# The output projection of a gated decoder trunk: a plain tiled product, or a fifth stage of seven block products

## The chip, the core and the metric

The kernel runs on one NeuronCore of a Trainium2 chip. Its engines work side by side and are joined by semaphores: TensorE (PE, matrix products; PEld are its weight loads), VectorE (DVE), ScalarE (ACT), GpSimd (POOL) and SyncE (SP), which mostly issues transfers. The core has 16 DMA engines. The metric is the device time of one execution in microseconds (us): the median of the runs.

## The reference, cut to what matters

The sizes are T = 1024 tokens and D = 1024 channels, in fp32.

```python
mod = c_act @ ada_w[l] + ada_b[l]
shift, scale, gate = jnp.split(mod, 3, axis=-1)
h = rms_norm(x, norm_w[l]) * (1.0 + scale[:, None, :]) + shift[:, None, :]
proj = h @ w_in[l]
...
u_h = y_h @ w_branch[l, 0]
u_g = y_g @ w_branch[l, 1]
mg = jax.nn.sigmoid(mg.reshape(B, T, N_BRANCH, D_MODEL))
merged = mg[:, :, 0] * u_h + mg[:, :, 1] * u_g
x = x + gate[:, None, :] * (merged @ w_out[l])
...
return rms_norm(x, final_norm_w)
```

## The kernel before, in words

Every large product is made in three passes: each fp32 operand is split into a rounded part `hi` and a remainder `lo` (ACT casts, DVE subtracts; `split`, L195 and L196), and `hi*hi + hi*lo + lo*hi` is summed in PSUM.

The first 820 us or so compute the input projection and the two attention branches. Then come four **product stages**, numbered b = 0 to 3, of 1024 x 1024 x 1024 each: stages 0 and 1 compute the two merge gates `mg`, stages 2 and 3 the branch projections `u_g` and `u_h`. Each is written as a two-by-two block product with seven products of 512 x 512 x 512 instead of eight (Winograd's form of Strassen's method), in the order of `PRODUCTS` (1, 2, 5, 3, 6, 7, 4). A product has four row blocks i, each one PSUM bank of 128 x 512, with 4 x 3 = 12 matmuls in `Pair.run` (L1399). Sums and differences of the blocks are needed as operands: those of the activations are made by DVE from four **quarters** (`load_quad`, `combine`, `build`; `build` also splits, L1319 and L1320); those of the weights are made long before in a side job and kept in DRAM (`weight_sums`), read back by `load_duo` (L1330) and split by `prep_duo` (L1341, L1342), two row blocks ahead. Partial results stay in PSUM banks a, e and b, with copies in SBUF.

After a row block, `Pair.after` hands results to the stage's output function. Stage 3's is `put_m`, which multiplies by the gate (L1491) and adds the other branch (L1494): `merged` is done, channels on partitions.

The **output projection** is a plain product: `make_m` splits the merged halves into `m_hi` and `m_lo`, called after each row block of stage 3; `OutBlk` (two of them, one per 512 output columns) loads `w_out`, splits it in `prep`, and in `run` computes eight row blocks of 24 matmuls (L1169, L1170, L1171). After each row block DVE multiplies the bank by the output gate `gate_b` (L1174), adds it to the row of x (L1176), and ACT squares and sums it (L1178); in the second half the root mean square is completed (L1184 to L1186), both halves are scaled (L1187, L1189) and stored (L1188, L1190).

The order of the work is set by a list of hooks, `at`, filled by `after(b, p, i, f)`: f runs, in program order, after row block i of product p in stage b. PE's, ACT's and DVE's instructions are then ordered ahead of the run from this program by the framework; on the chip each engine takes them strictly in that order. SP and POOL issue transfers in order too. SBUF outside of constants is 46 buffers of 4 KB per partition (`Slots`), taken and returned first in, first out; a transfer into a returned buffer waits until its last reader is done.

Of the kernel before, what the change touches and what calls it, by code (L numbers as in the profile page):

```python
# [15 lines left out]
P = 128  # L16
D = 1024
# [13 lines left out]
SUMS = {5: 0, 6: 1, 3: 2, 7: 3}  # L31

# [50 lines left out]
def hybrid_trunk_kernel(  # L83
# [1055 lines left out]
    class OutBlk:  # L1139


        def __init__(self, half):
            self.half, self.sl = half, slice(half * 512, half * 512 + 512)

        def load(self):
            self.raw = []
            for kk in range(4):
                b = S.get([2, 512])
                nc.sync.dma_start(b, w_out[0, kk * 256:(kk + 1) * 256, self.sl].rearrange("(k p) f -> p k f", p=P))
                self.raw.append(b)  # L1150

        def prep(self):
            self.wt = []
            for b in self.raw:
                self.wt.append(split(b))
                S.free(b)

        def run(self, at):
            half, sl = self.half, self.sl
            for n, t in enumerate((4, 5, 6, 7, 0, 1, 2, 3)):  # L1160
                if half == 0:
                    xr[t] = load_x(t)
                if n in at:
                    at[n]()
                po = R.get()
                for k in range(KT):
                    hi, lo = self.wt[k // 2]
                    lh, ll = m_hi[k][:, t * P:(t + 1) * P], m_lo[k][:, t * P:(t + 1) * P]
                    nc.tensor.matmul(po, lh, hi[:, k % 2, :], start=(k == 0), stop=False)  # L1169
                    nc.tensor.matmul(po, lh, lo[:, k % 2, :], start=False, stop=False)  # L1170
                    nc.tensor.matmul(po, ll, hi[:, k % 2, :], start=False, stop=(k == KT - 1))  # L1171
                r = xr[t][:, sl]
                tmp = xb_f[:, (n % 2) * 512:(n % 2) * 512 + 512]
                nc.vector.tensor_mul(tmp, po, gate_b[0][:, sl])  # L1174
                R.free(po)
                nc.vector.tensor_add(r, r, tmp)  # L1176
                junk = xb_f[:, 1024 + (n % 2) * 512:1024 + (n % 2) * 512 + 512]
                nc.scalar.activation(junk, r, AF.Square, accum_out=sso[:, t, half:half + 1])  # L1178
                f = fnw[0]
                if half == 0:  # L1180
                    nc.vector.tensor_mul(r, r, f[:, sl])
                else:
                    rs = rso[:, t:t + 1]
                    nc.vector.tensor_add(rs, sso[:, t, 0:1], sso[:, t, 1:2])  # L1184
                    nc.scalar.activation(rs, rs, AF.Sqrt, bias=eps_t, scale=1.0 / D)
                    nc.vector.reciprocal(rs, rs)  # L1186
                    nc.scalar.activation(xr[t][:, 0:512], xr[t][:, 0:512], AF.Copy, scale=rs)  # L1187
                    nc.sync.dma_start(o2[t * P:(t + 1) * P, 0:512], xr[t][:, 0:512])  # L1188
                    nc.vector.scalar_tensor_tensor(r, r, rs, f[:, sl], ALU.mult, ALU.mult)  # L1189
                    nc.sync.dma_start(o2[t * P:(t + 1) * P, 512:1024], r)  # L1190
            for hi, lo in self.wt:
                S.free(hi, lo)

# [261 lines left out]
    def half_of(store, d, half):  # L1458
        if d not in store:
            store[d] = S.get([T])  # L1460
        return store[d][:, half * 512:half * 512 + 512]

    gate0, gate1 = {}, {}
    gate1_d = [dp.tile([P, T], F32, name=f"gate1_{d}") for d in range(8)]
    m_hi, m_lo = [None] * 8, [None] * 8
# [7 lines left out]
    def put_gate0(d, half, ap, summed):  # L1473
        nc.scalar.activation(half_of(gate0, d, half), ap, AF.Sigmoid)
        if summed:
            Q.free(ap)
# [5 lines left out]
    def put_t1(d, half, ap, summed):  # L1482
        g = half_of(gate1, d, half)
        nc.vector.tensor_mul(g, g, ap)
        if summed:
            Q.free(ap)

    def put_m(d, half, ap, summed):
        sl = slice(half * 512, half * 512 + 512)
        g = gate0[d][:, sl]  # L1490
        nc.vector.tensor_mul(g, g, ap)  # L1491
        if summed:
            Q.free(ap)
        nc.vector.tensor_add(g, g, gate1[d][:, sl])  # L1494
        if d % 2 or half:
            later.extend([(d, 0)] if d % 2 == 0 else [])
            later.append((d, half))

    later = deque()
    made = {}  # L1500

    def make_m(leave=0):
        while len(later) > leave:
            d, half = later.popleft()
            if m_hi[d] is None:
                m_hi[d], m_lo[d] = S.get([T], F32R), S.get([T], F32R)
            sl = slice(half * 512, half * 512 + 512)
            split(gate0[d][:, sl], m_hi[d][:, sl], m_lo[d][:, sl])
            made[d] = made.get(d, 0) + 1
            if made[d] == 2:  # L1510
                S.free(gate0.pop(d), gate1.pop(d))
# [16 lines left out]
    for p in PRODUCTS[1:]:  # L1528
        for i in range(4):
            after(3, p, i, lambda: make_m(1))  # L1530
# [96 lines left out]
```

## Time and profile before

| what | value |
| --- | --- |
| median of 3 runs | 1237.3 us (1235.79 to 1238.61) |
| the profiled execution, its own time | 1236.45 us |
| its span, first to last instruction | 1234.7 us |
| PE / DVE / ACT / POOL busy | 1199.6 / 759.7 / 533.0 / 116.4 us |
| product stage 1 (about 903 to 980 us) | DVE 34.0, ACT 37.5 us busy in 77 us |
| product stage 3 (about 1057 to 1138 us) | DVE 71.9, ACT 38.7 us busy in 81 us |
| output projection (from about 1138 us) | DVE 44.4, ACT 26.1 us busy in the 97 us to the end |
| HBM read, written | 125.53 MB, 41.94 MB |

The views quoted below: busy shares of the whole span; stretches of time with each engine's busy time and the number of its instructions (x); the timeline, with an instruction's start and length and, in brackets, the engine's idle time before it and what ended it; groups of instructions by line; and the chain of waits, followed back from the end. A matmul's length in the timeline overlaps its neighbours, so their distance is read from the chain.

### The profile page before, as it was taken

The numbers are of one execution on the slowest core, as the hardware profiler recorded it, in microseconds if no ns is written. First come the engines' busy times: TensorE is split into PE (matmuls) and PEld (weight loads), VectorE is DVE, ScalarE is ACT, GpSimd is POOL, SyncE is SP. The second block draws the span as 40 slices with busy tenths as digits, with TensorE's granted clock in tenths as the row PEclk, the third lists the DMA queues.
The fourth block names the chain that finished last, engine by engine and source line by source line (L and its number), as shares of the span: only waits on it lengthen the run. The fifth ranks groups of instructions, "written<-read, shape, count | busy, mean of one in ns | idle before, by whom it ended". The sixth has DMA issues, their size and how long they took to land.

```text
span 1234.7 us, 20836 instructions
## 1 busy us (share of the span) xinstructions
PE 1199.6 (97%) x8627; PEld 992.4 (80%) x8627; DVE 759.7 (62%) x1225; ACT 533.0 (43%) x785; POOL 116.4 (9%) x201
## 2 busy tenths in 40 slices
PE   5999999999999999999999999999999999998997
PEld 3777889899898888788878878877888887787786
DVE  4636344765938375787774276785432668979443
ACT  5547723344444333424523233457543534454222
POOL 4100000202111121021010101101100000000000
PEclk9999999999999999999999999999999999999999
DMA  9714001746452367255151111345547456235202
GB/s 324 263 68 137 18 18 37 283 126 212 137 166 101 108 224 239 64 195 174 46 188 50 52 52 52 103 138 201 166 163 240 152 185 189 75 97 186 104 35 102
DMA packets 126928, 168.82 MB, mean 137 GB/s; under 512 B 7019, under 2 KB 97185, under 8 KB 126834
## 3 DMA queue, kind: packets, MB, share of 16 engines
q1 hardware_dynamic: 115234, 129.53, 33.5%
q0 software_dynamic: 11552, 37.97, 7.9%
q8 instruction: 67, 1.10, 0.4%
q14 instruction: 27, 0.22, 0.1%
q10 hardware_dynamic: 48, 0.01, 0.0%
HBM read 125.53 MB, written 41.94 MB: 136 GB/s over the span
## 4 chain that ended last, share of the span: by engine, by line
PE 54%; issue 24%; DVE 7%; DMA 3%; ACT 3%; POOL 2%; POOLq 0%; SPq 0%; DVEq 0%; ACTq 0%
PE pd L540 14%; PE pd L1399 8%; PE sc_ps L1399 5%; PE pm L1399 3%; PE pd L642 2%; PE pd L643 2%; PE pd L644 2%; DVE b L196 1%; PE pd L351 1%; PE pm L847 1%; PE pd L1169 1%; PE pd L1170 1%; PE pd L1171 1%; DMA b<-yh 1%; PE pm L828 1%
## 5 line engine op out<-in xcount | busy, mean ns | idle before, releaser
L540 PE MATMUL pd<-b,b 128*128 128x512 f32 x1632 | 387.5, 394 | 0.0
L540 PEld LDWEIGHTS pd<-b,b 128*128 128x128 f32 x1632 | 302.4, 188 | 64.9 <-issue 1.4
L1399 PE MATMUL pd<-b,b 128*128 128x512 f32 x720 | 175.5, 395 | 3.5 <-DVE b L952 1.5
L1399 PEld LDWEIGHTS pd<-b,b 128*128 128x128 f32 x720 | 134.5, 189 | 36.4 <-ACT b L1341 2.0
L196 DVE TENSOR_TENSOR b<-b,b 128x1024 fp32r<-128x1024 f32 (+2 forms) x99 | 102.4, 1045 | 84.9 <-ACT b L195 66.8
L195 ACT CAST b<-b 128x1024 fp32r<-128x1024 f32 (+2 forms) x99 | 86.5, 889 | 103.0 <-DVE b L1255 14.6
L1342 DVE TENSOR_TENSOR b<-b,b 128x1024 fp32r<-128x1024 f32 x56 | 68.2, 1222 | 70.0 <-ACT b L1341 54.1
L1341 ACT CAST b<-b 128x1024 fp32r<-128x1024 f32 x56 | 58.4, 1050 | 68.0 <-PE pd L1399 17.3
L1399 PE MATMUL sc_ps<-b,b 128*128 128x512 f32 x324 | 79.0, 391 | 1.2 <-ACT scT L792 1.2
L1399 PE MATMUL pm<-b,b 128*128 128x512 f32 x300 | 72.8, 390 | 3.3 <-DVE b L1342 3.3
L599 PE MATMUL pd<-b,b 128*128 128x256 f32 x256 | 74.2, 290 | 0.0
L601 PE MATMUL pd<-b,b 128*128 128x256 f32 x256 | 72.5, 283 | 0.0
L600 PE MATMUL pd<-b,b 128*128 128x256 f32 x256 | 72.4, 283 | 0.0
L1399 PEld LDWEIGHTS sc_ps<-b,b 128*128 128x128 f32 x324 | 60.4, 188 | 14.5 <-ACT scT L792 1.6
L1399 PEld LDWEIGHTS pm<-b,b 128*128 128x128 f32 x300 | 56.4, 188 | 15.4 <-DVE b L1342 3.7
L1320 DVE TENSOR_TENSOR b<-b,b 128x1024 fp32r<-128x1024 f32 x36 | 45.1, 1261 | 18.1 <-ACT b L1319 10.3
L351 PE MATMUL pd<-b,b 128*128 128x512 f32 x192 | 53.3, 410 | 1.6 <-ACT b L195 0.9
L1257 POOL DMA_DIRECT2D ws<-b x64 | 34.6, 541 | 192.9 <-DVE b L1251 86.9
L642 PE MATMUL pd<-b,b 128*128 128x512 f32 x128 | 51.3, 401 | 0.0
L734 ACT COPY xb<-b 128x512 f32<-128x512 f32 x48 | 29.4, 620 | 48.0 <-PE sc_ps L714 26.3
L643 PE MATMUL pd<-b,b 128*128 128x512 f32 x128 | 50.0, 390 | 0.0
L644 PE MATMUL pd<-b,b 128*128 128x512 f32 x128 | 49.9, 390 | 0.0
(269 smaller groups left out, 1991.3 us busy)
## 6 DMA issues: line engine op xcount, KB each, us to landing
b<-in_w_in_dram SPq DMA_DIRECT2D x66, 512.0 KB, 4.1
ws<-b POOLq DMA_DIRECT2D x64, 256.0 KB, 3.5
b<-ws SPq DMA_DIRECT2D x32, 512.0 KB, 4.5
b<-in_x_dram SPq DMA_DIRECT2D x16, 512.0 KB, 6.4
b<-in_ada_w_dram SPq DMA_DIRECT2D x32, 256.0 KB, 7.0
b<-in_w_branch_dram SPq DMA_DIRECT2D x16, 512.0 KB, 4.4
b<-h SPq DMA_DIRECT2D x14, 512.0 KB, 4.1
b<-in_w_in_dram SPq DMA_DIRECT2D x24, 256.0 KB, 4.2
```

The source lines that it names most:

```text
L195: nc.scalar.copy(hi, src)
L196: nc.vector.tensor_sub(lo, src, hi.bitcast(F32))
L351: nc.tensor.matmul(accs[f], wg(a, d, f), b[d][:, half * 512:half * 512 + 512], start=(d == 0 and n == 0), stop=(d == KT - 1 and n == 2))
L540: nc.tensor.matmul(ps[0:w, th * 512:(th + 1) * 512], a[:, k, 0:w], b[:, th * 512:(th + 1) * 512], start=(k == 0 and n == 0), stop=(k == KT ...
L599: nc.tensor.matmul(o, lh, hi[:, k % 4, :], start=(k == 0), stop=False)
L600: nc.tensor.matmul(o, lh, lo[:, k % 4, :], start=False, stop=False)
L601: nc.tensor.matmul(o, ll, hi[:, k % 4, :], start=False, stop=(k == KT - 1))
L642: nc.tensor.matmul(o, lh, hi[:, k % 2, :], start=(k == 0), stop=False)
L643: nc.tensor.matmul(o, lh, lo[:, k % 2, :], start=False, stop=False)
L644: nc.tensor.matmul(o, ll, hi[:, k % 2, :], start=False, stop=(k == KT - 1))
L1342: nc.vector.tensor_sub(lo, t, hi.bitcast(F32))
L1399: nc.tensor.matmul(o, a[:, sl], c, start=(p in (1, 5) and kt == 0 and n == 0), stop=(kt == 3 and n == 2), skip_group_check=True)
```

## The change

The output projection becomes product stage 4, with the same seven-product form, rows of tokens as PSUM rows and the order `OUT_PRODUCTS`. Its activations are the quarters that `put_m` leaves (`merged`), so `make_m`, `m_hi` and `m_lo` go, and `build` and `combine` are used on them from stage 3 on. Since the output gate multiplies columns of the result, it is moved into the weights: in stage 1 `load_wy` reads half of the rows of `w_out` at a time, `gate_wy` multiplies them by `gate_b`, `sum_wy` makes the four weight sums, and `keep_wy` writes all seven factors to DRAM (`w4_d`); `load_w4` and `prep_w4` bring them back and split them in stages 3 and 4. Each bank is added to rows of x or subtracted from them as soon as it holds a partial result (`out_after`). The removed class `OutBlk` and the functions `half_of` and `make_m` stand in the listing above.

```diff
+OUT_PRODUCTS = (1, 5, 3, 6, 7, 2, 4)
...
-    class OutBlk:
...
+    def merged(d, half):
+        pos = quads.setdefault((4, f"{d % 2 + 1}{half + 1}"), [None, None])
+        if pos[d // 4] is None:
+            pos[d // 4] = S.get([T])
+        return pos[d // 4][:, d // 2 % 2 * 512:d // 2 % 2 * 512 + 512]
...
     def put_m(d, half, ap, summed):
-        sl = slice(half * 512, half * 512 + 512)
-        g = gate0[d][:, sl]
+        g = merged(d, half)
         nc.vector.tensor_mul(g, g, ap)
         if summed:
             Q.free(ap)
-        nc.vector.tensor_add(g, g, gate1[d][:, sl])
-        if d % 2 or half:
-            later.extend([(d, 0)] if d % 2 == 0 else [])
-            later.append((d, half))
...
+        nc.vector.tensor_add(g, g, gate1[d][:, half * 512:half * 512 + 512])
+        if d % 2 != half:
+            S.free(gate1.pop(d))
...
-    for p in PRODUCTS[1:]:
-        for i in range(4):
-            after(3, p, i, lambda: make_m(1))
-
-    out0, out1 = OutBlk(0), OutBlk(1)
+
+    w4_d = {p: [dp.tile([P, T], F32, name=f"wo{p}{kk}") for kk in range(2)] for p in OUT_PRODUCTS}
+    w_rows = w_out[0].rearrange("(i two p) c -> two p i c", two=2, p=P)
+    wy, w4_raw, W4 = {}, {}, {}
+
+    def load_wy(kk):
+        for kh in range(2):
+            for f in range(2):
+                t = wy[kh, f] = S.get([2, 512])
+                nc.sync.dma_start(t, w_rows[kh][:, 2 * kk:2 * kk + 2, f * 512:f * 512 + 512])
+
+    def keep_wy(p, kk, kh, f):
+        nc.gpsimd.dma_start(w4_d[p][kk], wy[kh, f].rearrange("p a f -> p (a f)"))
+
+    def gate_wy(kk, n):
+        kh, f = ((0, 0), (0, 1), (1, 0), (1, 1))[n]
+        t = wy[kh, f]
+        nc.vector.tensor_mul(t, t, gate_b[0][:, f * 512:f * 512 + 512].unsqueeze(1).to_broadcast([P, 2, 512]))
+        for p, at_ in X_OF.items():
+            if at_ == (kh, f):
+                keep_wy(p, kk, kh, f)
...
+    def sum_wy(kk, n):
+        p, dst, other = ((7, (0, 0), (0, 1)), (5, (0, 1), (1, 1)), (6, (1, 1), (0, 0)), (3, (1, 0), (1, 1)))[n]
+        nc.vector.tensor_add(wy[dst], wy[dst], wy[other])
+        keep_wy(p, kk, *dst)
...
+    def load_w4(p):
+        w4_raw[p] = [S.get([2, 512]) for _ in range(2)]
+        for kk in range(2):
+            nc.sync.dma_start(w4_raw[p][kk].rearrange("p a f -> p (a f)"), w4_d[p][kk])
+
+    def prep_w4(p):
+        raw = w4_raw.pop(p)
+        W4[p] = list(zip(*[split(t) for t in raw]))
+        S.free(*raw)
...
+    def out_run(p, i):
+        if p in (1, 5):
+            bank4[BANK[p], i] = R.get()
+        o = bank4["c" if p == 2 else BANK[p], i]
+        h, w = H[4, p], W4[p]
+        for kt in range(4):
+            a_hi, a_lo = (z[kt // 2][:, kt % 2, i * P:(i + 1) * P] for z in h)
+            b_hi, b_lo = (z[kt // 2][:, kt % 2, :] for z in w)
+            for n, (a, b) in enumerate(((a_hi, b_hi), (a_hi, b_lo), (a_lo, b_hi))):
+                nc.tensor.matmul(o, a, b, start=(p in (1, 5) and kt == 0 and n == 0),
+                                 stop=(kt == 3 and n == 2), skip_group_check=True)
...
+    def first_columns(t, src):
+        squares(t, 0, src)
+        nc.vector.tensor_mul(xr[t][:, 0:512], src, fnw[0][:, 0:512])
+
+    def last_columns(t, bank):
+        r = xr[t][:, 512:1024]
+        nc.vector.tensor_add(r, r, bank)
+        squares(t, 1, r)
+        rs = rso[:, t:t + 1]
+        nc.vector.tensor_add(rs, sso[:, t, 0:1], sso[:, t, 1:2])
+        nc.scalar.activation(rs, rs, AF.Sqrt, bias=eps_t, scale=1.0 / D)
+        nc.vector.reciprocal(rs, rs)
+        nc.scalar.activation(xr[t][:, 0:512], xr[t][:, 0:512], AF.Copy, scale=rs)
+        nc.sync.dma_start(o2[t * P:(t + 1) * P, 0:512], xr[t][:, 0:512])
+        nc.vector.scalar_tensor_tensor(r, r, rs, fnw[0][:, 512:1024], ALU.mult, ALU.mult)
+        nc.sync.dma_start(o2[t * P:(t + 1) * P, 512:1024], r)
+
+    def out_after(p, i):
+        t = 4 + i
+        if p == 1:
+            snap4[i] = Q.get()
+            nc.scalar.activation(snap4[i], bank4["a", i], AF.Copy, scale=-1.0)
+            R.free(bank4.pop(("a", i)))
+        elif p == 5:
+            r = xr[t][:, 512:1024]
+            nc.vector.tensor_add(r, r, bank4["e", i])
+            b = bank4["b", i] = R.get()
+            nc.scalar.copy(b, snap4[i])
+        elif p == 3:
+            r = xr[t][:, 0:512]
+            nc.vector.tensor_sub(r, r, bank4["e", i])
+            R.free(bank4.pop(("e", i)))
+        elif p == 6:
+            r = xr[t][:, 0:512]
+            nc.vector.tensor_sub(r, r, bank4["b", i])
+            first_columns(t, r)
+        elif p == 7:
+            last_columns(t, bank4["b", i])
+            c = bank4["c", i] = R.get()
+            nc.vector.tensor_sub(c, xr[i][:, 0:512], snap4[i])
+            Q.free(snap4.pop(i))
+        elif p == 2:
+            first_columns(i, bank4["c", i])
+            R.free(bank4.pop(("c", i)))
+        elif p == 4:
+            last_columns(i, bank4["b", i])
...
+    for kk, (pa, pb) in enumerate(((5, 3), (6, 7))):
+        after(1, 2 if kk == 0 else 3, 3, lambda kk=kk: load_wy(kk))
+        for n in range(4):
+            after(1, pa, n, lambda kk=kk, n=n: gate_wy(kk, n))
+            after(1, pb, n, lambda kk=kk, n=n: sum_wy(kk, n))
...
+            (3, 3, 1, lambda: build((4, 1))),
+            (3, 7, 1, lambda: load_w4(1)),
+            (3, 4, 0, lambda: prep_w4(1)),
+            (3, 4, 1, lambda: load_w4(5)),
+            (3, 4, 2, lambda: load_rows(4, 5)),
+            (3, 4, 3, lambda: combine(4, "11", "12", "11")),
+            (4, 1, 0, lambda: build((4, 5))),
+            (4, 1, 0, lambda: load_rows(6, 7)),
+            (4, 1, 1, lambda: prep_w4(5)),
+            (4, 1, 1, lambda: load_w4(3)),
+            (4, 1, 2, lambda: combine(4, "12", "12", "22")),
+            (4, 5, 0, lambda: build((4, 3))),
+            (4, 5, 0, lambda: load_w4(6)),
+            (4, 5, 1, lambda: prep_w4(3)),
+            (4, 5, 2, last_of_11),
+            (4, 5, 3, load_norm_w),
+            (4, 3, 0, lambda: build((4, 6))),
+            (4, 3, 0, lambda: load_w4(7)),
+            (4, 3, 1, lambda: prep_w4(6)),
+            (4, 3, 2, lambda: load_rows(0, 1)),
+            (4, 6, 0, lambda: build((4, 7))),
+            (4, 6, 0, lambda: load_w4(2)),
+            (4, 6, 1, lambda: prep_w4(7)),
+            (4, 6, 1, lambda: load_rows(2, 3)),
+            (4, 6, 2, lambda: build((4, 2))),
+            (4, 7, 0, lambda: load_w4(4)),
+            (4, 7, 1, lambda: prep_w4(2)),
+            (4, 7, 3, last_of_22),
+            (4, 2, 0, lambda: build((4, 4))),
+            (4, 2, 1, lambda: prep_w4(4))):
...
-    make_m()
-    out0.run({1: out1.load, 3: out1.prep})
-    out1.run({})
+    out_stage()
```

The first table row of hooks reads: after row block 1 of product 3 in stage 3, build the first factor of stage 4.

More of the change, by code (lines that the diff above doesn't have):

```diff
@@ L1137, in hybrid_trunk_kernel @@
     fnw = [None]
-    class OutBlk:
[L1142 to L1192, printed above, removed]
@@ L1473, in put_gate0 @@
     def put_gate0(d, half, ap, summed):
[L1474 removed]
+        nc.scalar.activation(merged(d, half), ap, AF.Sigmoid)
         if summed:
@@ new lines, in out_stage @@
+    def out_stage():
+        for p in OUT_PRODUCTS:
+            for i in range(4):
+                out_run(p, i)
+                out_after(p, i)
+                for f in at.get((4, p, i), ()):
+                    f()
+            for z in H.pop((4, p)):
+                S.free(*z)
+            for z in W4.pop(p):
+                S.free(*z)
+    for kk, (pa, pb) in enumerate(((5, 3), (6, 7))):
[3 more added lines that the diff above has]
+            after(1, pb, n, lambda kk=kk, n=n: sum_wy(kk, n))
```

46 lines of the change are left out of this document (24 added, 22 removed).

## The prediction

> **What bounds the kernel now.** I read the page's busy shares first, then the stretches by engine, then the timeline where TensorE loses time.
>
> ```profile
> span 1234.7 us, 20836 instructions
> PE 1199.6 (97%) x8627; PEld 992.4 (80%) x8627; DVE 759.7 (62%) x1225; ACT 533.0 (43%) x785; POOL 116.4 (9%) x201
> ```
>
> TensorE (PE) is busy 97% of the span; no other engine is above 62%. So matmuls taken away should come off the end, if the vector engine (DVE) and the transfers keep up in the places where work is put. The whole-run shares don't tell that; the stretches do (columns: length, then busy time and instruction count of each engine, granted clock, DMA share, GB/s).
>
> ```profile
> core 0: us, PE busy (x) PEld busy (x) DVE busy (x) ACT busy (x) POOL busy (x), PEclk, DMA share, GB/s
> 1110.00:1120.00 10.00, 10.00 (x45) 8.26 (x44) 10.00 (x15) 5.20 (x8) 0.00 (x0) 1.00 0.78 260
> 1120.00:1130.00 10.00, 6.69 (x28) 4.93 (x27) 10.00 (x17) 6.85 (x9) 0.00 (x0) 0.96 0.01 4
> 1130.00:1140.00 10.00, 10.00 (x39) 8.15 (x40) 9.91 (x14) 2.88 (x4) 0.00 (x0) 0.87 0.74 233
> 1140.00:1150.00 10.00, 9.10 (x41) 7.21 (x40) 8.17 (x10) 4.19 (x6) 0.00 (x0) 1.00 1.00 396
> 1150.00:1170.00 20.00, 20.00 (x89) 16.07 (x88) 8.31 (x12) 2.90 (x8) 0.00 (x0) 1.00 0.01 2
> ```
> ```profile
> 1094.46 8.16 PE pd L1399 x36
> 1116.37 2.91 PE L1399 MATMUL pd<-b,b 128*128 128x512 f32 x12
> 1119.53 1.05 ACT L1341 CAST b<-b 128x1024 fp32r<-128x1024 f32 x1 [2.17 <-DMA b<-in_w_branch_dram]
> 1127.92 1.21 DVE L1342 TENSOR_TENSOR b<-b,b 128x1024 fp32r<-128x1024 f32 x1
> 1129.19 0.79 PE L1399 MATMUL pm<-b,b 128*128 128x512 f32 x1 [3.31 <-DVE b L1342]
> 1129.79 4.33 PE L1399 MATMUL pd<-b,b 128*128 128x512 f32 x12
> ```
>
> From the chain, 36 matmuls advance in 8.16 us: 0.2267 us each. The 30 us from 1120 hold 28 + 39 + 41 = 108 matmuls, worth 24.5 us, so **5.5 us are lost** there, at the border between the fourth product stage and the output projection. The cause is visible: DVE is full, the second half of a weight split (L1342) runs at 1127.92 though its first half (ACT, L1341) ended at 1120.6, and PE stands 3.31 us for it. The next twelve matmuls then take 4.33 instead of 2.91, at a mean clock of 0.87: the stall costs about 3.3 + 1.4 = 4.7 us.
>
> That clock row is also what the Trainium skill describes (TensorE: Matmul & The Clock Gate, Part 1: The HAM clock gate): an idle window of about 3.4 us halves the clock until the array has been busy as long. The trace agrees in kind. By the rule a stall clearly below that window costs only itself, and term 2 below would be 1.4 smaller; the sum goes by the row.
>
> What fills DVE there:
>
> ```profile
> L196 DVE TENSOR_TENSOR b<-b,b 128x512 fp32r<-128x512 f32 (+1 forms) x19 | 15.2, 820 | 0.1
> 1111.37 1.14 DVE b L1342
> 1112.51 0.60 DVE b L1494
> ```
>
> In 1100 to 1140 DVE spends 15.2 us on L196: splits of the merged activations (512 columns) and of the output weights (1024). Back to back, DVE advances 0.60 us for an operation of 512 columns and 1.14 us for one of 1024; I use these below.
>
> **Term 1, the matmuls.**
>
> ```profile
> L1169 PE MATMUL pd<-b,b x64: 388/389/504, 1125.0 to 1216.3; 128*128 128x512 f32 x64
> L1169 PE MATMUL sc_ps<-b,b x32: 389/389/500, 1124.8 to 1194.2; 128*128 128x512 f32 x32
> L1169 PE MATMUL pm<-b,b x32: 388/389/389, 1166.4 to 1226.3; 128*128 128x512 f32 x32
> ```
>
> L1169 to L1171 issue 128 each, 384 in all. The new stage issues 7 products x 4 row blocks x 4 x 3 = 336, of the same shape and with the same kind of operands. 48 x 0.2267 = **-10.9 us**, all on the path. The weight load under each (PEld) is unchanged.
>
> **Term 2, the border stall.** Removed between 1100 and 1140: sixteen splits of 512 columns (ACT and DVE) and four of the output weights, 16 x 0.60 + 4 x 1.14 = 14.2 us of DVE. In their place come, up to the border, the new first factor (build (4,1), 2.3), its weights (2.3) and one difference (2.3): 6.9 us. The product stage's own DVE work stays: per border product (6 and 7) 12 x 0.60 for outputs, 2.28 for weight splits, 2.28 for a factor and, in 6, 2.28 for a difference: 14.0 and 11.8 us against 48 x 0.2267 = 10.9 of PE; in product 4 8 x 0.60 plus 4.6 new = 9.4. DVE falls at most 4.0 us behind and is 2.5 behind at the border, under the 5.4 us (two row blocks) by which weight splits run ahead. Also the first three new products (1, 5, 3) read quarters that are finished before product 4, so nothing at the border waits for the last output. I take the whole loss back: **-5.4**, bounds -5.4 and 0; a gain beyond, up to -3.5, from the small losses in 1057 to 1120, where more buffers are free, enters the low end only.
>
> **Term 3, the new stage itself.** DVE per product, with the moved builds, splits and differences (2.28 each): product 1: three of these, 6.8 in 10.9 us of PE; product 5: three and four adds, 9.2; product 3: two and four subtractions, 7.0; product 6: three and eight halves, 11.6; product 7: two, four subtractions into the new banks and four row ends (0.60 + 0.75 + two tiny), about 13; product 2: two and four halves, 7.0; product 4: four row ends. The 2.5 us brought in are gone within product 1. In 6 and 7 DVE falls 2.8 us behind; the splits for 2 stand early in 7, and what is late is the factor for product 4, with 10.9 - 7.0 = 3.9 us of room in product 2. It just fits. A row end waits twice for ACT (bracketed below), 1.2 us each, and if none of that is filled 4 x 1.2 more breaks the room: bounds 0 and two stalls like the one above, 9.4; nearest row: the full DVE of 1110 to 1120, which did 10.00 of 10, so the waits are filled; I take **+1.5**. ACT gets 28 splits of 1.05, 29.4 us in 76, and the squares and eight copies of banks beside them. Weight loads (14 of 512 KB) and rows of x come through SP at least a product ahead, and behind them on SP stand only later loads and the stores; from 1150 the DMA was empty (share 0.01), which covers them.
>
> **Term 4, the second gate stage**, in which the weights are multiplied and summed.
>
> ```profile
> 920.00:930.00 10.00, 10.00 (x46) 8.29 (x45) 2.34 (x3) 4.25 (x6) 0.00 (x0) 1.00 0.73 249
> 930.00:940.00 10.00, 10.00 (x45) 8.28 (x45) 1.52 (x2) 2.12 (x3) 0.00 (x0) 1.00 0.66 224
> 940.00:950.00 10.00, 10.00 (x45) 8.26 (x44) 3.05 (x3) 3.26 (x5) 0.00 (x0) 1.00 0.58 170
> 950.00:960.00 10.00, 10.00 (x46) 8.28 (x45) 5.68 (x7) 7.13 (x10) 0.00 (x0) 1.00 0.86 289
> 960.00:970.00 10.00, 10.00 (x46) 8.29 (x45) 10.00 (x11) 6.41 (x8) 0.00 (x0) 1.00 0.61 189
> 970.00:980.00 10.00, 10.00 (x46) 8.29 (x45) 5.57 (x6) 5.72 (x8) 0.00 (x0) 1.00 0.46 142
> 980.00:990.00 10.00, 10.00 (x46) 8.28 (x45) 4.32 (x5) 5.89 (x8) 0.00 (x0) 1.00 0.32 107
> 990.00:1000.00 10.00, 10.00 (x46) 8.29 (x45) 8.50 (x11) 3.51 (x4) 0.00 (x0) 1.00 0.31 99
> L1298 DVE TENSOR_TENSOR b<-b,b x8: 1214/1218/1226, 1012.5 to 1053.9; 128x1024 f32<-128x1024 f32 x8
> 904.87 0.54 POOL L1470 DMA_DIRECT2D gate<-b  x1 [3.15 <-ACT b L1469]
> ```
>
> DVE: sixteen operations of 1024 columns; half repeat an operand along the row as L1298 does, at the usual 1.22 us. 16 x 1.22 = 19.5 us in 60 of which 28.2 are busy. Only around 960 to 970 is it full already; four sums (4.6 us) fall there, under the 5.4 us of lead. DMA: 8 loads and 14 stores of 512 KB, 11.5 MB; at 396 GB/s (the row with share 1.00) 29.1 us of full DMA. Free in 920 to 980 are 60 x (1 - 0.65) = 21.0, so 8.1 us run over into 980 to 1000, which has 13.7 free. Nothing is lost unless a load comes too late: bounds 0 and 8.1. The new waits: DVE waits for the four loads; behind it stand the weight splits that PE needs. SP: eight more issues, behind them the loads of the next weights. POOL: 14 issues at 0.54; the row quoted is its last before these stretches, in which it does nothing. By the code's list of buffers eleven or more are free there, and the loads take four. I take **+1.0**.
>
> The Trainium skill speaks against the change here (DMA: Bandwidth & Descriptors, Specifications): about 358 GB/s of HBM per core, with which the 11.5 MB would be 32 us and the overflow 11. The trace's 396 GB/s is above it, and decides.
>
> **Term 5, the end.**
>
> ```profile
> 1226.76 0.39 PE L1171 MATMUL pm<-b,b 128*128 128x512 f32 x1
> 1227.19 0.69 DVE L1174 TENSOR_TENSOR xb<-pm,b 128x512 f32<-128x512 f32 x1 [1.70 <-PE pm L1171]
> 1229.45 0.16 DVE L1184 TENSOR_TENSOR rso<-sso 128x1 f32<-128x1 f32 x1 [0.85 <-ACT xb L1178]
> 1229.97 0.16 DVE L1186 RECIPROCAL rso<-rso 128x1 f32<-128x1 f32 x1 [0.36 <-ACT rso L1185]
> 1230.17 0.75 DVE L1189 SCALAR_TENSOR_TENSOR b<-b,rso,b 128x512 f32<-128x512 f32 x1
> ```
>
> The gate's multiplication (L1174) leaves every row end: -0.7. But row ends now come every 12 matmuls (2.72 us), not 24, and the chain from L1174's successor to the end of L1189 is 3.7 - 0.7 = 3.0 us; four in a row may lag 3 x 0.28 = 0.85. Together **+0.1**, bounds -0.7 and +0.9.
>
> **Sum.** -10.9 - 5.4 + 1.5 + 1.0 + 0.1 = -13.7. The profiled execution took 1236.45 (span 1234.7 and 1.75 around it), which gives 1222.75; the median of the runs is 0.85 above it: **1223.6 us**. Its own range, by terms 3 to 5: 1219 to 1229.
>
> **Rivals.**
>
> The old stall keeps its place. For it: DVE is 95% full over 1100 to 1140 and the order of DVE is fixed before the run; against it: 7.3 us less work there. 1223.6 + 5.4 = 1229.0, and with one further stall of 4.7 in products 6 to 4, 1233.7. Chance 0.19.
>
> DMA becomes the bound in the second gate stage: the 8.1 us of overflow land on the path instead of my 1.0: 1230.7. For it the shares of 0.58 to 0.86; against it that PE lost nothing there though 0.86 was reached. Chance 0.06.
>
> Slower than before: DVE's order puts the factors and weight splits of the new stage behind its outputs, so that PE stalls at each of its six product borders as at 1129, 4.7 us each: 28.2 in place of 1.5, 1250.3. It decides from the fourth border on (15.2 / 4.7 = 3.2). For it: exactly this happened once, and products 6 and 7 have more DVE work than PE work; against it: the five other products have less, and the factors are asked for a product ahead. Chance 0.12.
>
> The change doesn't save what it says: seven products are fewer matmuls only if they run as dense as the plain loop. Holes of 0.5 us in each of the 28 row blocks (14 us) would leave 1237. Against it: the four stages before run so at 0.2267 us. Chance 0.03.
>
> **How the numbers follow.** Forecast 0.60. Faster by over 0.2% (2.5 us; smaller differences a measurement of this kernel can't tell from none): forecast, first and second rival, 0.85. Same 0.03, slower 0.12. The range leaves out the third and fourth rival and some hundredths: its top, 1235, holds both faster rivals; its bottom is 1237.3 - 10.9 - 5.4 - 0.7 - 3.5 = 1217.
>
> **What would show it.** Right: 336 matmuls in the last stage at 0.2267 us, about 76 us from its first to its last; no wait of PE over 1 us between product 6 of the fourth stage and product 5 of the new one; the second gate stage still 76 to 77 us long with DMA shares near 1; about 7.5 us from the last matmul to the end. Wrong: PE waiting for L1320's, L1342's or L196's successors at the borders 7/2 and 2/4 of the new stage; PE waiting for weight splits in the second gate stage, with DVE in turn waiting for a DMA; a last stage longer than 85 us.

## The result, and the profile after

| | before | after |
| --- | --- | --- |
| median | 1237.62 us (4 runs, 1235.79 to 1238.61) | 1231.03 us (4 runs, 1230.16 to 1231.72) |
| ratio | | 0.9948, 95% interval 0.9931 to 0.9965 |
| profiled execution, its span | 1236.45, 1234.7 us | 1230.16, 1228.3 us |

The change makes the kernel 6.6 us faster, about half of the 13.7 that were forecast. The page's first lines, and the waits of PE from the second gate stage to the end (us in total, times, longest):

```profile
span 1228.3 us, 20868 instructions
...
PE 1187.6 (97%) x8579; PEld 984.7 (80%) x8579; DVE 791.6 (64%) x1245; ACT 547.1 (45%) x797; POOL 123.7 (10%) x215
```
```profile
PE sc_ps L1342 <- DVE b L1329: 12.2, 1, 12.2
```

PE has 48 matmuls fewer, as the change says, and is busy 97% as before. But one wait of 12.2 us is new. L1342 is now the matmul of the product stages and L1329 (`Pair.summed`, stage output) the operation of DVE that it waits for. To see what was won and lost where, I laid both timelines at two landmarks in unchanged code, short groups of four matmuls in product stages 0 and 3. Before, then after with its last matmuls:

```profile
892.57 1.07 PE L1399 MATMUL pm<-b,b 128*128 128x512 f32 x4
1102.46 1.07 PE L1399 MATMUL pm<-b,b 128*128 128x512 f32 x4
```
```profile
891.07 1.07 PE L1342 MATMUL pm<-b,b 128*128 128x512 f32 x4
951.01 2.88 PE L1342 MATMUL pm<-b,b 128*128 128x512 f32 x12
966.05 5.49 PE L1342 MATMUL sc_ps<-b,b 128*128 128x512 f32 x12 [12.16 <-DVE b L1329]
1114.27 1.07 PE L1342 MATMUL pm<-b,b 128*128 128x512 f32 x4
1217.91 2.88 PE L1517 MATMUL pd<-b,b 128*128 128x512 f32 x12
```

| stretch | before | after | difference |
| --- | --- | --- | --- |
| start to the landmark in stage 0 | 892.57 | 891.07 | -1.5 (unchanged code) |
| to the landmark in stage 3 | 209.89 | 223.20 | +13.3 |
| to the start of the last matmul | 124.30 | 106.13 | -18.2 |
| to the end of the span | 7.94 | 7.90 | 0.0 |

(The last matmul of after starts at 1217.91 + 11 x 0.2267 = 1220.40.) The last stages give 18.2 us, more than the 14.8 net of the forecast's terms 1, 2 and 3. The stretch with the second gate stage takes 13.3 back: the wait of 12.16, and 5.49 - 2.88 = 2.61 by which the next twelve matmuls are slower. The other small losses of this stretch (912 matmuls, worth 206.75 us) fell from 3.1 to 1.7, which leaves 13.3.

The last stage and the border into it, after (lines of 1144 to 1228, then the stretches):

```profile
L1517 PE MATMUL pd<-b,b 128*128 128x512 f32 x168 | 39.5, 389 | 0.0
L1517 PE MATMUL sc_ps<-b,b 128*128 128x512 f32 x96 | 23.1, 390 | 0.0
L1517 PE MATMUL pm<-b,b 128*128 128x512 f32 x72 | 17.3, 389 | 0.0
```
```profile
930.00:940.00 10.00, 10.00 (x46) 8.28 (x45) 3.96 (x4) 1.68 (x3) 1.31 (x3) 1.00 1.03 393
940.00:950.00 10.00, 10.00 (x46) 8.29 (x45) 7.08 (x6) 1.05 (x1) 1.59 (x3) 1.00 1.01 368
950.00:960.00 10.00, 3.89 (x18) 2.88 (x16) 2.36 (x2) 0.59 (x1) 1.06 (x2) 0.90 1.03 383
960.00:970.00 10.00, 3.95 (x9) 3.17 (x10) 5.33 (x6) 4.96 (x8) 0.00 (x0) 0.50 0.46 162
...
1120.00:1130.00 10.00, 10.00 (x45) 8.26 (x44) 9.98 (x14) 6.04 (x7) 0.00 (x0) 1.00 0.93 318
1130.00:1140.00 10.00, 10.00 (x46) 8.28 (x45) 10.00 (x15) 3.06 (x3) 0.00 (x0) 1.00 0.49 170
1140.00:1150.00 10.00, 10.00 (x45) 8.16 (x44) 10.00 (x13) 6.49 (x7) 0.00 (x0) 1.00 0.66 207
```

The new stage has its 168 + 96 + 72 = 336 matmuls and no idle time before any of them. The three stretches from 1120 hold 45 + 46 + 45 = 136 matmuls where before had 108: 28 more, worth 6.3 us, although DVE is busy 29.98 of these 30 us and was busy 28.08. The four stretches from 930 are the other side: the DMA is full (shares 1.01 to 1.03) for 30 us, PE does 18 and 9 matmuls in the last two of them in place of 46, and the granted clock falls to 0.50.

What stood in the way there is on the timelines of ACT and DVE:

```profile
945.44 1.05 ACT L1284 CAST b<-b 128x1024 fp32r<-128x1024 f32 x1 [12.69 <-DMA b<-ws]
959.41 1.99 ACT L1284 CAST b<-b 128x1024 fp32r<-128x1024 f32 x2 [12.92 <-DMA b<-in_w_branch_dram]
961.31 0.59 ACT L1316 ACTIVATE b<-sc_ps 128x512 f32<-128x512 f32 x1
```
```profile
904.17 1.23 DVE L1473 TENSOR_TENSOR b<-b,b 128x1024 f32<-128x1024 f32 x1
...
954.11 1.23 DVE L1482 TENSOR_TENSOR b<-b,b 128x1024 f32<-128x1024 f32 x1 [4.14 <-DMA wo<-b]
963.04 2.36 DVE L1285 TENSOR_TENSOR b<-b,b 128x1024 fp32r<-128x1024 f32 x2 [6.57 <-DMA wo<-b]
965.31 0.68 DVE L1329 TENSOR_TENSOR b<-b,sc_ps 128x512 f32<-128x512 f32 x1
```

Read them from below. PE's product 7 starts at 966.05, right behind L1329 (965.31 and 0.68 long): L1329 reads the bank beside the one that product 7 writes, in the same tile of two banks (`sc_ps`), and the program makes PE wait for it. The low half of product 7's own first weights, the second of the two L1285, was done only 0.6 us before. L1329 needs the copy L1316 of ACT. The last row block of product 6 starts at 951.01, so the first, three times 12 x 0.2267 earlier, started at about 942.9 and was there to copy at about 945.6; the copy ran at 961.31, because a cast that stands ahead of it in ACT's order waited 12.92 us for a transfer. That transfer is `in_w_branch`, which product stage 1 does not read: it holds the weights of the next stage. DVE, before L1329, stands 6.57 us up to 963.04, until a store of the output weights (`wo`) into DRAM has left a buffer; it also needed the first of the two casts, which ended at 960.45, so the store alone is the last 2.6 of these. And the sixteen new operations (L1473, L1482) all ran between 904 and 955, while the last four sums have their hooks beside product 7, which started at 966.

ACT's instructions of the changed kernel in their fixed order, by number, with the numbers of their buffers:

```
521 L1284 CAST b592<-b578 128x1024   (product 7, row blocks 2 and 3)
522 L1284 CAST b618<-b604 128x1024   (in_w_branch: stage 2, product 1, row blocks 2 and 3)
523 L1284 CAST b584<-b569 128x1024   (product 7, row blocks 0 and 1)
524 L1316 ACTIVATE b579<-sc_ps 128x512
```

Row 522 is the misplaced one. Its DVE half stands likewise ahead of L1329, where it writes into the buffer that the store has to leave. The two parts of the transfer behind it were issued at 947.74 and 949.20, after all the loads of the output weights, the last of which went out at 933:

```profile
947.74 0.86 SPq L1277 DMA_DIRECT2D b<-in_w_branch_dram  x1
949.20 1.00 SPq L1277 DMA_DIRECT2D b<-in_w_branch_dram  x1
```

They also went out late. Ahead of them SP, which issues in order, stood 8.3 us for a subtraction of DVE (L1285, 945.22 to 946.44), and on DVE that one stood behind an early multiplication, which had to wait itself:

```profile
942.82 1.22 DVE L1473 TENSOR_TENSOR b<-b,b 128x1024 f32<-128x1024 f32 x1 [8.86 <-PE pm L1342]
```

### The profile page after: what moved, and what is told of

The parts are those of the page before. It is cut to its first block, busy times and chain, and to the rows that moved or that the text cites. A ratio compares the mean times of both kernels' runs of the same rounds, so it can differ in the third digit from the quotient of the medians.

```text
span 1228.3 us, 20868 instructions
## 1 busy us (share of the span) xinstructions
PE 1187.6 (97%) x8579; PEld 984.7 (80%) x8579; DVE 791.6 (64%) x1245; ACT 547.1 (45%) x797; POOL 123.7 (10%) x215
## 4 chain that ended last, share of the span: by engine, by line
PE 51%; issue 29%; DVE 6%; POOL 3%; ACT 3%; DMA 3%; POOLq 0%; SPq 0%; DVEq 0%; ACTq 0%
PE pd L541 14%; PE pd L1342 7%; PE sc_ps L1342 4%; PE pm L1342 3%; PE pd L1517 3%; PE pd L643 2%; PE pd L645 2%; PE pd L644 2%; PE sc_ps L1517 2%; PE pd L352 1%; PE pm L848 1%; PE pm L1517 1%; PE pm L829 1%; PE pm L850 1%; POOL gate L1414 1%
## 5 line engine op out<-in xcount | busy, mean ns | idle before, releaser
L541 PE MATMUL pd<-b,b 128*128 128x512 f32 x1632 | 387.8, 394 | 0.0
L1342 PE MATMUL pd<-b,b 128*128 128x512 f32 x720 | 173.6, 392 | 2.4 <-DVE b L953 1.5
L1342 PEld LDWEIGHTS pd<-b,b 128*128 128x128 f32 x720 | 134.2, 188 | 33.3 <-DVE b L953 1.9
L197 DVE TENSOR_TENSOR b<-b,b 128x1024 fp32r<-128x1024 f32 (+2 forms) x89 | 99.1, 1124 | 83.4 <-ACT b L196 66.1
L196 ACT CAST b<-b 128x1024 fp32r<-128x1024 f32 (+2 forms) x89 | 82.9, 948 | 92.2 <-DVE b L1198 14.4
L1285 DVE TENSOR_TENSOR b<-b,b 128x1024 fp32r<-128x1024 f32 x56 | 68.4, 1224 | 52.2 <-ACT b L1284 19.6
L1342 PE MATMUL sc_ps<-b,b 128*128 128x512 f32 x324 | 81.8, 401 | 12.9 <-DVE b L1329 12.2
L1284 ACT CAST b<-b 128x1024 fp32r<-128x1024 f32 x56 | 58.3, 1049 | 75.5 <-PE pd L1342 19.1
L1342 PEld LDWEIGHTS sc_ps<-b,b 128*128 128x128 f32 x324 | 61.9, 193 | 27.4 <-DVE b L1329 12.6
L1263 DVE TENSOR_TENSOR b<-b,b 128x1024 fp32r<-128x1024 f32 x48 | 59.5, 1254 | 21.7 <-ACT b L1262 14.3
L1342 PE MATMUL pm<-b,b 128*128 128x512 f32 x300 | 72.1, 389 | 0.0
L1262 ACT CAST b<-b 128x1024 fp32r<-128x1024 f32 x48 | 50.0, 1049 | 38.5 <-PE pd L1342 17.0
L1342 PEld LDWEIGHTS pm<-b,b 128*128 128x128 f32 x300 | 56.3, 188 | 11.7
L352 PE MATMUL pd<-b,b 128*128 128x512 f32 x192 | 53.2, 409 | 1.7 <-ACT b L196 0.9
L643 PE MATMUL pd<-b,b 128*128 128x512 f32 x128 | 51.3, 401 | 0.0
L644 PE MATMUL pd<-b,b 128*128 128x512 f32 x128 | 49.9, 390 | 0.0
```

Of the source, the lines that this page charges most:

```text
L196: nc.scalar.copy(hi, src)
L197: nc.vector.tensor_sub(lo, src, hi.bitcast(F32))
L352: nc.tensor.matmul(accs[f], wg(a, d, f), b[d][:, half * 512:half * 512 + 512], start=(d == 0 and n == 0), stop=(d == KT - 1 and n == 2))
L541: nc.tensor.matmul(ps[0:w, th * 512:(th + 1) * 512], a[:, k, 0:w], b[:, th * 512:(th + 1) * 512], start=(k == 0 and n == 0), stop=(k == KT ...
L643: nc.tensor.matmul(o, lh, hi[:, k % 2, :], start=(k == 0), stop=False)
L644: nc.tensor.matmul(o, lh, lo[:, k % 2, :], start=False, stop=False)
```

## The experiments

The theory: the sixteen operations run earlier than their hooks, this packs 11.5 MB of transfers into 50 us, and late transfers hold ACT and DVE ahead of the urgent copies. Against it stood: the number of bytes alone; the early release of the `wy` buffers; the sums done in place, which wait for the store of their own buffer; and the length of the added DVE work.

**The sixteen operations kept at their place in the program** (`keep_in_program_order` leaves an instruction behind all that precedes it on its engine in the program).

```diff
-        nc.vector.tensor_mul(t, t, gate_b[0]...)
+        tc.keep_in_program_order(nc.vector.tensor_mul(t, t, gate_b[0]...))
...
-        nc.vector.tensor_add(wy[dst], wy[dst], wy[other])
+        tc.keep_in_program_order(nc.vector.tensor_add(wy[dst], wy[dst], wy[other]))
```

> The sixteen multiplications and sums of the output weights stay behind the DVE work that precedes them in program order, so they no longer run up to two products early. All bytes and all waits for stores remain. If the loss of about 14.6 us in the second gate stage (12.2 us of PE standing, 2.6 us of slow clock after it) comes from that early order, which packs the 11.5 MB into 905 to 957 us and puts the sums ahead of what product 6 and 7 need: PE stands under 2 us there, DMA share stays under 0.95 in most slices, time 1215 to 1219 us. If the bytes alone hold PE, wherever they are put: 5 us or more remain, 1221 us or above.

Measured: 1221.09 us (1218.96 to 1223.82), ratio to before 0.9881 (0.9860 to 0.9902). PE in 903 to 980, and the largest wait of PE left behind it:

```profile
903.00:980.00 77.00, 77.00 (x342) 63.77 (x341) 44.41 (x42) 33.37 (x45) 7.99 (x15) 1.00 0.92 327
```
```profile
PE pd L1342 <- ACT b L1418: 2.3, 1, 2.3
```

The 12.2 us are gone with the order alone, with every byte and operation kept. Two parts of the expectation missed: the DMA is still full (1.07 in 940 to 950), and the time is 2 us above the range and just inside that of the other reading, 2.3 of it the wait above and 0.8 another, at 983 to 988. The 5 us of PE wait that the other reading asks for are not there: PE has no idle time in these 77 us. In the order of this kernel the cast of row 522 also stands elsewhere, so it does not tell the sums from the cast; the last experiment does.

**Buffers released a product later; then also sums in buffers of their own.**

```diff
         if n == 3:
-            S.free(*wy.values())
+            held.append(list(wy.values()))
             wy.clear()
...
+    def drop_held():
+        S.free(*held.pop(0))
...
+    after(1, 6, 3, drop_held)
+    after(1, 4, 3, drop_held)
```
```diff
-        nc.vector.tensor_add(wy[dst], wy[dst], wy[other])
+        total = S.get([2, 512])
+        nc.vector.tensor_add(total, wy[dst], wy[other])
+        spent.append(wy[dst])
+        wy[dst] = total
...
+            held.append([*wy.values(), *spent])
```

> Only one thing is changed: the four weight buffers of each half are given back a product later (after 1,6,3 and 1,4,3), so that no weight split is written into a buffer whose store to DRAM is still running. Bytes, order of the sums and their own waits for stores stay. Theory A (waits on stores: splits into buffers just stored, and sums in place): the 6.6 us wait of DVE for a store before the split goes, PE stands under 4 us, 1218 to 1222 us. Theory B (the full DMA brings the loads of weights late): PE still stands 8 us or more, 1227 us or above.

> As the run before, and the sums are written to buffers of their own, so that DVE waits for no store at all. Bytes and early order stay. Theory A: no wait of DVE for a store, PE stands under 2 us, 1215 to 1219 us. Theory B: the loads are still late, PE stands 8 us or more, 1227 us or above.

Measured: 1226.35 us (1224.57 to 1228.21), ratio 0.9922 (0.9902 to 0.9943), and 1226.11 us (1222.49 to 1229.56), ratio 0.9920 (0.9892 to 0.9948). The wait of PE in each, with the twelve matmuls behind it:

```profile
960.17 5.41 PE L1342 MATMUL sc_ps<-b,b 128*128 128x512 f32 x12 [4.55 <-DVE b L1329]
```
```profile
964.48 5.89 PE L1342 MATMUL pd<-b,b 128*128 128x512 f32 x12 [3.39 <-ACT b L1284]
```

12.16 falls to 4.55 and, with no store for DVE to wait for, to 3.39. Neither side of either expectation was met. But these edits also moved the order. The copy L1316 in each kernel, and what held PE up there:

```profile
947.50 0.60 ACT L1316 ACTIVATE b<-sc_ps 128x512 f32<-128x512 f32 x1 [1.89 <-PE sc_ps L1342]
957.16 1.23 DVE L1482 TENSOR_TENSOR b<-b,b 128x1024 f32<-128x1024 f32 x1 [6.10 <-DMA wo<-b]
```
```profile
947.53 0.60 ACT L1316 ACTIVATE b<-sc_ps 128x512 f32<-128x512 f32 x1 [3.25 <-PE sc_ps L1342]
959.79 1.05 ACT L1284 CAST b<-b 128x1024 fp32r<-128x1024 f32 x1 [7.41 <-DMA b<-in_w_in_dram]
```

In both, L1316 waits for PE alone and runs some 14 us earlier: the cast of row 522 no longer stands ahead of it. So these two runs can't tell the held buffers from the shifted order. What they show is what is left without that cast: in the first an early sum that waits for a store ahead of L1329; in the second, where L1329 is in time, a cast for product 4 (`in_w_in`) that waits 7.41 us for its load, ahead of a cast that product 7 needs.

**Stores cut to 16 of 1024 columns** (stage 4 then reads rows of `w_out`).

```diff
-        nc.gpsimd.dma_start(w4_d[p][kk], wy[kh, f].rearrange("p a f -> p (a f)"))
+        nc.gpsimd.dma_start(w4_d[p][kk][:, 0:16], wy[kh, f][:, 0, 0:16])
...
-            nc.sync.dma_start(w4_raw[p][kk]..., w4_d[p][kk])
+            nc.sync.dma_start(w4_raw[p][kk]..., w_out[0, p * P:(p + 1) * P, :])
```

> Leaves out nearly all bytes of the fourteen stores (16 columns of 1024 are written), and the new stage reads rows of w_out in their place, as many bytes as before. All DVE work, its early order, the number of stores and the waits on them stay. A and B both: stores end in about 2 us and the DMA is not full, PE stands under 2 us, about 1215 to 1218 us. A third theory, C, that the 19.5 us of DVE work put early hold PE by their own length: PE still stands 8 us or more.

One time, 1217.33 us, and in the second gate stage:

```profile
903.00:980.00 77.00, 77.00 (x340) 63.46 (x339) 50.41 (x47) 35.84 (x49) 8.07 (x15) 1.00 0.70 236
949.47 2.00 ACT L1284 CAST b<-b 128x1024 fp32r<-128x1024 f32 x2 [4.98 <-DMA b<-in_w_branch_dram]
954.36 0.68 DVE L1329 TENSOR_TENSOR b<-b,sc_ps 128x512 f32<-128x512 f32 x1
955.70 2.88 PE L1342 MATMUL sc_ps<-b,b 128*128 128x512 f32 x12
```

The early order and all of DVE's operations are kept, the misplaced cast still stands ahead of L1316, and PE does not wait: the cast waits 4.98 us in place of 12.92, and L1329 ends 0.7 us before PE comes to product 7. So the length of the DVE work is no cause, and this early order does harm only together with the bytes of the stores: the DMA share over these 77 us is 0.70 here and 0.92 in the first experiment, which moves them all.

**The work spread over both gate stages**, half in stage 0 and half in stage 1, with the order kept by hand and without.

```diff
-    for kk, (pa, pb) in enumerate(((5, 3), (6, 7))):
-        after(1, 2 if kk == 0 else 3, 3, lambda kk=kk: load_wy(kk))
+    for kk in range(2):
+        after(kk, 1, 3, lambda kk=kk: load_wy(kk))
         for n in range(4):
-            after(1, pa, n, lambda kk=kk, n=n: gate_wy(kk, n))
-            after(1, pb, n, lambda kk=kk, n=n: sum_wy(kk, n))
+            after(kk, 2, n, lambda kk=kk, n=n: gate_wy(kk, n))
+            after(kk, 5, n, lambda kk=kk, n=n: sum_wy(kk, n))
```

> Half of the weight work goes to the first gate stage (loads after 0,1,3, multiplications beside product 2, sums beside product 5) and the other half to the same places of the second; the sixteen operations are kept in program order. If late bytes behind a full DMA are what remains of the loss in the pinned kernel: no wait of PE over 1 us in either gate stage, no slice of 10 us with a DMA share above 0.95 in 903 to 980 us, time 1215 to 1219 us, below the pinned kernel by 2 to 5 us. If instead the remainder is not the DMA: as the pinned kernel, about 1221 us.

> The same spread without keeping the order. If room on the DMA is enough by itself, the early order harms nothing: within 2 us of the run before, no PE wait over 1 us. If the early order costs by itself: PE stands 3 us or more in one of the gate stages, 1221 us or above.

Measured: with the order kept 1219.82 us (1219.4 to 1220.38), ratio 0.9867 (0.9853 to 0.9882), the best version here and ahead of both kernels; without 1222.13 us (1221.52 to 1225.66), ratio 0.9892 (0.9872 to 0.9911). Their largest waits of PE in the gate stage:

```profile
936.42 3.03 PE L1342 MATMUL sc_ps<-b,b 128*128 128x512 f32 x12 [1.82 <-ACT b L1314]
```
```profile
933.66 4.62 PE L1342 MATMUL pm<-b,b 128*128 128x512 f32 x12 [3.87 <-ACT b L1418]
```

The expectation for the first was a little too good (one wait of 1.8 in the second gate stage and one of 1.1 in the first, a share of 1.02 in 920 to 930, 0.8 us above the range). Spreading is worth 1.3 us over keeping the order alone, with intervals that overlap, not the 2 to 5 that were expected. With half of the bytes in this stage the free order still makes a wait of 3.9 us, behind a cast of ACT that waited 6.90 us for a load, and the medians differ by 2.3 with ranges apart. That is no cost of the order by itself: the DMA is full there for a while as well (0.99 in 920 to 930).

**Order kept and buffers held**, the first two edits together.

> The pinned order, and the four weight buffers given back a product later. The pinned kernel still showed ACT 3.45 us behind a store and PE 3.0 us behind ACT at the end of the second gate stage. If those came from splits into buffers whose store still ran: they go, 1217 to 1219 us. If they came from late loads: they stay, 1220 to 1222 us.

1224.19 us (1223.03 to 1225.46), ratio 0.9902 (0.9884 to 0.9921): outside both ranges, its median 3 us above that with the order alone, though the intervals overlap. PE waits once more, at a later place:

```profile
988.07 4.32 PE L1342 MATMUL sc_ps<-b,b 128*128 128x512 f32 x12 [2.81 <-ACT pd L1325]
```

That the held buffers make later loads wait would explain it; it was not followed further.

**The kernel before, without the low half of `merged`** (the DVE subtraction of each split in `make_m` is left out, and the high half is used in place of the low).

> The kernel before; leaves out the DVE subtraction for the low part of merged (16 operations of 512 columns; the high part is used in its place), ACT's casts, buffers and matmuls stay. If DVE's load makes the border stall (term 2): the wait of PE for L1342 of 3.3 us goes, most of the 5.5 us come off, about 1231 to 1233 us. If it is the order or the buffers: the wait stays, about 1236 us.

One time, 1229.85 us, beside a median of 1235.71 of the kernel before and 1.2 us below the range that was expected. The wait of 3.31 us for L1342 at the border is not there; the largest left in the last stages is

```profile
PE sc_ps L1169 <- DVE xb L1174: 2.3, 1, 2.3
```

So the old stall goes with these subtractions, as the prediction read it. The order of DVE's and ACT's other operations at the border changes with them, so whether DVE's load or its order made the stall is not told apart.

**The one misplaced split alone kept in place**: row 522 and its DVE half.

```diff
     def prep_duo(*duo):
-        nc.scalar.copy(hi, t)
-        nc.vector.tensor_sub(lo, t, hi.bitcast(F32))
+        (tc.keep_in_program_order if duo == (2, 1, 1) else lambda i: i)(nc.scalar.copy(hi, t))
+        (tc.keep_in_program_order if duo == (2, 1, 1) else lambda i: i)(nc.vector.tensor_sub(lo, t, hi.bitcast(F32)))
```

> The changed kernel, with one weight split alone kept at its place in the program: that of the next stage's first product, second half (its ACT cast and its DVE subtraction). The fixed order had put it, on ACT and on DVE, just ahead of the cast and subtraction for product 7 and of the bank copy L1316 and the output L1329 for which PE stands 12.2 us; it now comes some twenty instructions later on ACT. All sixteen operations on the output weights stay early, and the DMA as full as before (share above 1.0 in 930 to 960). Theory A: this one misplaced split, whose weights were loaded behind the packed transfers (issued at 949.20) and whose low buffer waits for a store of wo, carries most of the wait; PE stands under 6 us there and the time is 1221 to 1226. Theory B: what is late is the packed DMA itself, whatever stands in the order: product 7's own weights, next in ACT's order, come as late; PE stands 9 us or more, and the time is 1229 to 1232.

1222.63 us (1222.15 to 1225.18), ratio 0.9881 (0.9852 to 0.9909). ACT, DVE and PE around the place:

```profile
950.08 2.00 ACT L1284 CAST b<-b 128x1024 fp32r<-128x1024 f32 x2 [12.53 <-DMA b<-ws]
951.99 0.59 ACT L1316 ACTIVATE b<-sc_ps 128x512 f32<-128x512 f32 x1
```
```profile
957.68 1.23 DVE L1482 TENSOR_TENSOR b<-b,b 128x1024 f32<-128x1024 f32 x1 [3.08 <-DMA wo<-b]
958.83 2.35 DVE L1285 TENSOR_TENSOR b<-b,b 128x1024 fp32r<-128x1024 f32 x2
961.10 0.68 DVE L1329 TENSOR_TENSOR b<-b,sc_ps 128x512 f32<-128x512 f32 x1
```
```profile
940.00:950.00 10.00, 10.00 (x46) 8.28 (x45) 2.51 (x3) 0.00 (x0) 0.07 (x1) 1.00 1.04 413
961.84 4.61 PE L1342 MATMUL sc_ps<-b,b 128*128 128x512 f32 x12 [3.76 <-DVE b L1329]
```

Two instructions moved, and the wait falls from 12.16 to 3.76 with the DMA about as full as before (1.04, and 0.95 in 950 to 960). That is the first reading, by PE's wait and by the time. With the slower matmuls behind it the stall falls from 14.8 to 3.76 + 1.73 = 5.5, by 9.3; the medians differ by 8.4 and the ratios to the kernel before by 0.67%, 8.3 us. The second reading, that product 7's own weights come as late as the others, falls: they were there by 950. What is left shows its cause as well: the copy L1316 is done at 952.6, and L1329 runs at 961.10, behind an early sum that waits for a store. Keeping the sums at their hooks removes that (the first experiment), though its ratio, 0.9881 as here, is no better: other waits of 2.3 and 0.8 us came up there.

## Why the prediction was half right

**Term 1, the matmuls (-10.9): right.** 336 of the same 0.2267 us, without a hole. The rival in which holes eat the saving falls.

**Term 2, the border (-5.4): right, and more.** The last stretch gave 18.2; less term 1 this leaves 7.3: 6.4 between 1120 and 1150, and 0.9 behind. The prediction read 5.5 in the same 30 us because a matmul on the edge of two stretches counts in both: 104 matmuls start there, not 108, and 30 less 104 x 0.2267 is 6.4. A wait of 0.9 us for L1174 at 1145.90, in the old output projection, is among them. The small losses between 1057 and 1120, which the prediction put into the low end alone, are no part of this: 1.5 of their 1.6 us stand before the landmark, in the stretch whose small losses fell by 1.5. That the stall goes with the DVE work of the splits holds by the experiment on the kernel before; load and order were not told apart. The margin reckoned there held too: DVE was full to 9.98 and 10 of 10 from 1120 to 1150, and PE had no wait. The rival in which the old stall keeps its place falls (DVE was 97% full from 1100 to 1140 of the kernel before, 38.70 of 40 us, where it says 95%).

**Term 3, the new stage (+1.5): 0.** No product border of it stalls, so the rival that ended slower than before falls. The estimate that 7 to 13 us of DVE per product just fit was on the safe side.

**Term 5, the end (+0.1): right.** 7.94 and 7.90 from the last matmul's start to the end. The last row's chain starts at 1221.40, right behind the last matmul, and its store is issued at 1224.81:

```profile
1221.40 0.68 DVE L1533 TENSOR_TENSOR b<-b,pd 128x512 f32<-128x512 f32 x1
1224.81 0.38 SPq L1542 DMA_DIRECT2D out_dram<-b  x1
```

**Term 4, the second gate stage (+1.0, at most 8.1): this is the step that failed.** It measured 14.8. The mechanism named was near (late loads, and DVE waiting for a DMA with weight splits behind it, stands under what would be wrong), but the term rests on two assumptions that did not hold.

First, it placed the sixteen operations at their hooks, the sums around 960 to 970, and set the lead of two row blocks, 5.4 us, against them. But the prediction itself says that DVE's order is fixed before the run, and a fixed order may pull work forward. The first multiplication ran at 904.17, some 20 us ahead of its hook (two products before product 6, product 5 starts at 942.9 - 2 x 10.9 = 921.1, and its first row block ends at 923.8), the last sum before product 7 had begun.

Second, it took the bytes that run over, 8.1 us, as the most that could land on PE's path. That is a bound where the late transfer itself is what PE needs. Here it was one that nothing needed for some 20 us, but its split stood in the order of two engines ahead of what PE waited for. How long the wait got was set by when that one transfer was issued and by when it landed behind everything issued before it, not by the overflow of bytes; and it paid the slow clock on top, 2.6 us. The rival that made DMA the bound (1230.7) comes out near the measured time, 1231.0, but for another reason: it kept the other terms as forecast, while they gave more; the place was right and its 8.1 was not.

What each cause carries of the 14.8, with the split taken away first: the one misplaced split 9.3, the early sums behind a store the other 5.5. The sums alone, with the split left where it is, were not tried. Both need the bytes of the stores, without which the same early order cost nothing (one run).

Together the terms measured -10.9 - 7.3 + 0 + 14.8 + 0; with -1.5 of small losses before the landmark and -1.5 in code that the change doesn't touch, this is the -6.4 between the two profiled spans.

Why the framework chose this order was not tried. That it counts with transfers quicker than a full DMA gives them fits what is seen, and is no more than argued.

## What to carry to other kernels

Work that is "hidden" beside a busy engine is hidden only if each instruction of it that waits for a transfer stands behind, in its engine's order, all that the busy engine needs meanwhile; so look up the order that will be run, not the place in the program, before costing a moved step. When an engine waits for a transfer, look whose data it is: if nothing nearby uses it, the order is at fault, and keeping a single split in its place can be worth most of the stall. And bound a late transfer by when it is issued and when it lands behind the full queues, not by the bytes that are over. An experiment that adds or removes operations can move this order too, so look where the suspect instruction stands in each run before reading its time.

## What the runs showed of the hardware

**Under a full DMA one kind of load took almost three times as long.** Issues of 905 to 985 in after, and one kind in 900 to 980 of before for comparison (number, KB each, median us from issue to landing):

```profile
wo<-b POOLq DMA_DIRECT2D x14, 512.0 KB, 7.0
b<-yg SPq DMA_DIRECT2D x8, 512.0 KB, 11.2
```
```profile
b<-yg SPq DMA_DIRECT2D x8, 512.0 KB, 3.9
```

The same loads take 11.2 us where they took 3.9. Not every kind suffers so: in the same two views `in_w_in` goes from 3.9 to 7.1 and `gate` from 4.8 to 5.4, but `ws` from 5.8 to 5.2 and `in_w_branch` from 4.4 to 3.5. The stretches with shares of 1.01 to 1.04 moved 368 to 413 GB/s, again above the figure of about 358 that the Trainium skill has for HBM per core (DMA: Bandwidth & Descriptors, Specifications).

**The price of a short PE stall has a step.** Twelve matmuls take 2.88 us. Behind waits of 1.82 and 2.28 us they took 3.03 and 3.06; behind 2.81, 3.31, 3.76 and 3.87 us 4.32, 4.33, 4.61 and 4.62; behind 4.55 and 12.16 us 5.41 and 5.49, and behind one of 3.39 us 5.89 (there the low half of a split, done 1.2 us after the first matmul, adds to it). The recorded clock is at half for 3.41 us in each of the four cases in the middle, for 6.83 us behind 3.39 and 4.55, and for 13.65 us about the wait of 12.16; the rows 0.96 and 0.87 of the kernel before, 0.8 and 2.6 us at half, add up to the same 3.4. The long ones agree with the Trainium skill (TensorE: Matmul & The Clock Gate, Part 1: The HAM clock gate), by which an idle window of about 3.4 us halves the clock: twelve matmuls take nearly twice as long, and the clock row of 960 to 970 says 0.50. But a wait of 2.81 us, shorter than that window, already cost 1.4 us more than itself, and the step in these runs lies between 2.3 and 2.8.

**A full DVE is no stall by itself.** From 1120 to 1150 it was busy 29.98 of 30 us, in the kernel before 29.91 from 1110 to 1140, and PE lost nothing where it had lost 6.4. What counted may be whether the next split stood early enough in its order; that is not shown.
